# A hybrid decoder layer: the feed-forward parts, the values and the output projection with tokens held in the matmul engine

## The chip, the cores and the metric

The kernel runs on one core of a Trainium2 chip. The metric is the device time of one execution in microseconds (us). The engines are TensorE (PE; its weight loads stand as PEld), VectorE (DVE), ScalarE (ACT), GpSimd (POOL) and SyncE (SP), which issues the DMAs here. The inputs, all in f32, lie in the chip's memory.

## The reference

One layer for 256 tokens of width 1024. A vector `c` gives, by a 1024 x 9216 matrix (`ada`), nine rows of 1024: shift, scale and gate for each of three blocks. The blocks are a SwiGLU feed-forward part of width 2816 (FFN1, with half a step), a mixer and a second feed-forward part (FFN2).

```
def rmsnorm(x, g):  return x * rsqrt(mean(x * x, -1) + EPS) * g
def modulate(h, shift, scale):  return h * (1 + scale) + shift
def swiglu(h, w_gate, w_up, w_down):  return (silu(h @ w_gate) * (h @ w_up)) @ w_down
...
proj = h @ w_in                       # q, k, v of 512 columns each, x_m and z of 512 each
o_a = rmsnorm(attention of 8 heads of 64)
o_m = (norm of an mLSTM of 4 heads of 128 + skip * conv) * silu(z)
return concatenate([o_a, o_m]) @ w_out
```

Each block is x + gate * block(modulate(rmsnorm(x))), the gates of the feed-forward parts halved; a last norm with `final_norm` follows.

## The kernel before, in words

**Weights.** All weights come once, as 1 MB chunks of 128x2048 in four buffers named `raw`. `load_to` issues their DMAs on SyncE's queue, three chunks ahead of use (`weights(ahead=3)`). Each chunk is cut in pieces of 1024 columns, and each piece is split in two parts: ScalarE writes the rounded `whi`, VectorE the rest, `wlo = raw - whi` (`split_piece`), one chunk ahead of use. Five buffers hold each part.

**Products.** Activations are kept with features on the partitions, as `hh` and `hl` (rounded and rest). `mm3` makes a product of three matmuls: `whi` with `hh`, `wlo` with `hh`, `whi` with `hl`. A 128x128 block of the weights rests in TensorE, and 256 columns, the tokens, pass through. The result has features on the partitions and tokens along the columns.

**Norms.** `residual` adds a block's result to x by features (one piece of 128 features x 256 tokens at a time), squares it, and makes the next `hh` and `hl` at once with `pre_h`, without the norm's factor. The factor, one number per token, is made meanwhile from sums of squares over the partitions by a plain f32 matmul with ones (`rstd_of`), and is multiplied in behind the next product (`finish_pre`, `shifted`, `conv`). The shift passes through the product as two more columns (W = 258 columns, `pre_shift`).

**FFN.** Gate and up columns are produced tile by tile (22 tiles of 128), the gated product `gm` is split in `gh` and `gl`, and the down projection makes 8 tiles of 128 features, each a sum over 22 blocks.

**Adaptive rows.** The 72 columns of `c @ ada` are made on VectorE: a 128x1024 tile `ada` is loaded (three buffers) and multiplied with the broadcast `c_bc` with a running sum (`junk<-ada,c_bc`). The first 16 come before FFN1, the others are put in one by one with `side`: `QF` and `QD` say how many by chunk in FFN1's gate/up and down parts.

**Order.** DMAs on SyncE and the loads of ScalarE's tables stand as written. The order of the other engines is set by the tile framework's scheduler, which moves instructions by its own timeline; each engine then runs its list in order, and waits are by semaphore.

## Time and profile before

| | us |
|---|---|
| median of three runs | 546.89 |
| lowest and highest | 544.8, 547.9 |
| the profiled execution | 544.78 |
| its span | 543.0 |
| FFN1 gate/up, full stretch | 41.8 to 147.4 |
| FFN1 down | 147.4 to 209.8 |
| mixer | 209.8 to 313.7 |
| output projection | 313.7 to 338.6 |
| FFN2 gate/up | 338.6 to 469.7 |
| FFN2 down | 469.7 to 531.9 |
| tail | 531.9 to 543.0 |

A stretch's busy time of an engine is to be held against the stretch's length: where TensorE's equals it, TensorE sets the pace, and other engines' waits cost nothing. A matmul's recorded duration is its latency, and matmuls overlap; the pace is the distance from one start to the next, or the chain's length over its count. In a group of several records, the time runs from the first start to the last end.

### The profile page before, as it was taken

The page shows a single profiled execution, that of the slowest core. Times are in us where ns is not written, and L with a number is a line of the kernel's source. Part 1 is how long each engine was busy: PE and PEld are TensorE (multiplying, and loading weights), DVE is VectorE, ACT ScalarE, POOL GpSimd, SP SyncE. Part 2 cuts the span into 40 slices and gives each one's busy share as a digit, 9 for nine tenths or more (in the row PEclk, how much of TensorE's full clock was granted, in tenths as well). Part 3 has the DMA queues.
Part 4 walks back from the last instruction along what each step waited for, and adds up shares of the span by engine and source line. Part 5 has one row for each costly group of instructions (what it writes and reads, how often), then busy time and mean ns, then how long its engine had stood idle before and what let it go on. Part 6 is the DMA issues. An engine that isn't in the chain of part 4 may idle for free.

```text
span 543.0 us, 10281 instructions
## 1 busy us (share of the span) xinstructions
PE 520.8 (96%) x4172; PEld 502.2 (92%) x4172; DVE 419.6 (77%) x712; ACT 281.6 (52%) x486; POOL 48.8 (9%) x64
## 2 busy tenths in 40 slices
PE   7799999899999999999999979999999999999992
PEld 7799999899999999988977779999999999999992
DVE  7989879999889887998965286989987777644423
ACT  4455346456655345366767554875554554544410
POOL 4000000000001010210000030400000000023221
PEclk9999999999999999999999989999999999999998
DMA  8998987879779889579621114387856455455002
GB/s 312 341 415 324 367 307 299 319 305 332 295 278 320 326 278 348 216 269 349 228 79 59 31 73 150 124 354 278 316 182 218 160 172 217 156 189 200 1 0 77
DMA packets 23953, 125.76 MB, mean 232 GB/s; under 512 B 2657, under 2 KB 2913, under 8 KB 14434
## 3 DMA queue, kind: packets, MB, share of 16 engines
q1 hardware_dynamic: 23906, 125.11, 62.5%
q8 instruction: 32, 0.52, 0.4%
q14 instruction: 15, 0.12, 0.1%
HBM read 124.05 MB, written 1.05 MB: 230 GB/s over the span
## 4 chain that ended last, share of the span: by engine, by line
PE 90%; DVE 5%; DMA 2%; ACT 1%; issue 1%; SPq 0%; DVEq 0%; ACTq 0%
PE psa L54 42%; PE psb L54 26%; PE psm L54 22%; DVE junk L54 2%; DMA raw<-in_gu 1%; DMA x<-in_x 1%; DVE wlo L54 1%; DVE u_out L54 0%; ACT whi L54 0%; DVE nw L54 0%; DVE oa L54 0%; ACT sq L54 0%; SPq L97 0%; DVEq L1080 0%; DVE rr L54 0%
## 5 line engine op out<-in xcount | busy, mean ns | idle before, releaser
L54 ACT ACTIVATE whi<-raw 128x1024 fp32r<-128x1024 f32 (+1 forms) x162 | 169.2, 1048 | 137.5 <-PE psa L54 65.1
L54 DVE TENSOR_TENSOR wlo<-raw,whi 128x1024 fp32r<-128x1024 f32 (+1 forms) x162 | 196.2, 1215 | 53.3 <-ACT whi L54 52.2
L54 PE MATMUL psa<-hh,whi 128*128 128x258 f32 (+1 forms) x396 | 110.4, 283 | 0.6 <-DVE gm L54 0.6
L54 PE MATMUL psa<-hh,wlo 128*128 128x258 f32 (+1 forms) x396 | 110.5, 283 | 0.0
L54 PE MATMUL psa<-hl,whi 128*128 128x258 f32 (+1 forms) x396 | 109.4, 283 | 0.0
L54 PE MATMUL psb<-hh,whi 128*128 128x258 f32 (+1 forms) x320 | 92.1, 289 | 4.3 <-ACT whi L54 2.4
L54 DVE SCALAR_TENSOR_TENSOR junk<-ada,c_bc 128x1024 bf16<-128x1024 f32 x72 | 87.7, 1218 | 8.9 <-DMA ada<-in_ada 8.7
L54 PE MATMUL psb<-hh,wlo 128*128 128x258 f32 (+1 forms) x320 | 90.5, 284 | 1.2 <-DVE wlo L54 1.2
L54 PE MATMUL psb<-hl,whi 128*128 128x258 f32 (+1 forms) x320 | 90.0, 284 | 0.0
L54 PEld LDWEIGHTS psa<-hh,whi 128*128 128x128 f32 x396 | 74.4, 189 | 0.8 <-DVE gm L54 0.8
L54 PEld LDWEIGHTS psa<-hh,wlo 128*128 128x128 f32 x396 | 74.4, 189 | 0.0
L54 PEld LDWEIGHTS psa<-hl,whi 128*128 128x128 f32 x396 | 74.0, 190 | 0.0
L54 PEld LDWEIGHTS psb<-hh,whi 128*128 128x128 f32 x320 | 60.4, 189 | 6.8 <-ACT whi L54 3.0
L54 PEld LDWEIGHTS psb<-hh,wlo 128*128 128x128 f32 x320 | 60.3, 189 | 2.0 <-DVE wlo L54 1.4
L54 PEld LDWEIGHTS psb<-hl,whi 128*128 128x128 f32 x320 | 60.3, 190 | 0.0
L54 PE MATMUL psm<-hh,wlo 128*128 128x256 f32 (+1 forms) x204 | 57.4, 283 | 0.0
L54 PE MATMUL psm<-hh,whi 128*128 128x256 f32 (+1 forms) x204 | 57.3, 283 | 0.0
L54 PE MATMUL psm<-hl,whi 128*128 128x256 f32 (+1 forms) x204 | 57.0, 283 | 0.0
L54 PE MATMUL psa<-gh,whi 128*128 128x256 f32 x176 | 49.5, 281 | 0.0
L54 PE MATMUL psa<-gh,wlo 128*128 128x256 f32 x176 | 49.5, 281 | 0.0
L54 PE MATMUL psa<-gl,whi 128*128 128x256 f32 x176 | 49.4, 281 | 0.0
L54 PEld LDWEIGHTS psm<-hh,whi 128*128 128x128 f32 x204 | 38.5, 189 | 0.1
(235 smaller groups left out, 903.8 us busy)
## 6 DMA issues: line engine op xcount, KB each, us to landing
ada<-in_ada SPq DMA_DIRECT2D x72, 512.0 KB, 5.8
raw<-in_dn SPq DMA_DIRECT2D x22, 1024.0 KB, 4.8
raw<-in_guB SPq DMA_DIRECT2D x19, 1024.0 KB, 4.7
raw<-in_gu SPq DMA_DIRECT2D x18, 1024.0 KB, 6.4
raw<-in_gu SPq DMA_DIRECT2D x8, 512.0 KB, 7.3
raw<-in_wqk SPq DMA_DIRECT2D x4, 1024.0 KB, 5.6
raw<-in_wout SPq DMA_DIRECT2D x4, 1024.0 KB, 7.9
raw<-in_guA SPq DMA_DIRECT2D x4, 768.0 KB, 4.4
```

Source lines behind the costliest of these rows:

```text
L54: r = f(*a, **k)
```

## The change

In the feed-forward parts, the values and the output projection the roles are turned: `mx3` rests a block of 128 features x 128 tokens (`tok`) in TensorE, and 512 columns of weights pass through. The result has tokens on the partitions. The products of q, k, x_m and z stay as `mm3`, with 256 columns instead of 258.

- x is kept by tokens (`xt`, two tiles of 128 x 1024; `turn_x` makes them with transposes). `residual` multiplies a 128x512 result by the gate as a row and adds; ScalarE sums the squares along the row. `row_norm` makes the factor per token with a power on GpSimd. `normed` makes y = x * factor * scale row + shift row, and `to_h` turns y by transposes and splits it in `hh` and `hl`. The norm's factor is thus applied ahead of the products of the mixer and FFN2.
- The gated product comes by tokens too (`gated`), and `turn` transposes it into `gh` and `gl`.
- The gate, scale and shift rows and the final norm are written to a scratch in memory (`row_of`, 128x8x1) and read back broadcast over the partitions (`load_row`, 128x1024).
- The columns of the down weights are regrouped: a chunk holds 4 or 2 row blocks x 512 columns (`down`, SIZES) and is loaded in four or five DMAs of 256 KB or less. Some pairs of gate/up chunks and the values' chunks are loaded in two DMAs each.
- In FFN1's down part 24 of the `ada` jobs run (16 before): QF, QD = (1, 0, 1), (2, 0, 0).

The core of the diff:

```diff
+    def by_row(g, d):
+        def pieces(raw):
+            v = raw.rearrange("p (g d c) -> p d g c", g=g, d=d)
+            n = d * 1024 // raw.shape[-1]
+            return [v[:, k:k + n] for k in range(0, d, n)]
+        return pieces
...
+    def down(src, dg, a, n):
+        def moves(raw):
+            r = []
+            for k in range(4):
+                b, o = (4 * dg + k) * NF + a, k * n * P
+                while o < (k + 1) * n * P:
+                    m = min((k + 1) * n - o // P, 16 - b % 16)
+                    r.append((raw[:, o:o + m * P], src[b // 16][:, b % 16 * P:(b % 16 + m) * P]))
+                    b, o = b + m, o + m * P
+            return r
+        return 4 * n * P, moves, by_row(4, n)
+    SIZES = [4, 4, 4, 2, 4, 4]
+    def downs(src):
+        return [down(src, dg, sum(SIZES[:k]), n) for dg in range(2) for k, n in enumerate(SIZES)]
...
+    def mx3(ps, xh, xl, hi, lo, start, stop):
+        pe.matmul(ps, xh, hi, start=start, stop=False, skip_group_check=True)
+        pe.matmul(ps, xh, lo, start=False, stop=False, skip_group_check=True)
+        pe.matmul(ps, xl, hi, start=False, stop=stop, skip_group_check=True)
...
+    def row_of(src, name):
+        scr = scratch[name] = drm.tile([ND, P], F32, name=nm("scr"), tag=nm("scr"))
+        later.append((jobs_run[0] + 1, lambda: dma(scr.rearrange("j p -> p j"), src)))
+    def run_later(all=False):
+        while later and (all or later[0][0] <= jobs_run[0]):
+            later.pop(0)[1]()
+    def load_row(name, tag):
+        rows[name[:2]] = const([P, D], F32, "row", tag=tag)
+        dma(rows[name[:2]], scratch[name].rearrange("j p -> (j p)").partition_broadcast(P))
...
-    def pre_h(k, d):
-        act.activation(hh[:, d, 0:T], x_sb[:, d], AF.Copy, scale=gs[k][:, d:d + 1])
-        dve.scalar_tensor_tensor(hl[:, d, 0:T], x_sb[:, d], gs[k][:, d:d + 1], as32(hh[:, d, 0:T]),
-                                 ALU.mult, ALU.subtract)
-    def pre_shift(k):
-        for c in range(2):
-            act.activation(hh[:, :, T + c], sh[k], AF.Copy)
-            dve.tensor_tensor(hl[:, :, T + c], sh[k], as32(hh[:, :, T + c]), ALU.subtract)
...
-    def residual(d, ps, g, k):
-        dve.scalar_tensor_tensor(x_sb[:, d], ps, g[:, d:d + 1], x_sb[:, d], ALU.mult, ALU.add)
-        if k is None:
-            s = add_sq(d, pool)
-            pool.tensor_scalar(fin_u[0][:, d], x_sb[:, d], sm[:, C_NF + d:C_NF + d + 1], None, ALU.mult)
-            return s
-        if d == ND - 1:
-            s = add_sq(d, pool)
-            pre_h(k, d)
-        else:
-            pre_h(k, d)
-            s = add_sq(d, pool)
-        return s
-    fin_u = [None]
...
+    def residual(k, tt, dg, ps):
+        c = slice(dg * 512, dg * 512 + 512)
+        t = t512("rt")
+        x = xt[tt][:, c]
+        dve.tensor_tensor(t, ps, rows["gt"][:, c], ALU.mult)
+        dve.tensor_tensor(x, x, t, ALU.add)
+        n = 4 * k + 2 * tt + dg
+        t2 = tmp.tile([P, 512], BF16, tag="sq5", name=nm("sq5"), bufs=1)
+        act.activation(t2, x, AF.Square, accum_out=ss[:, n:n + 1])
+    def row_norm(k, tt):
+        n, m = 4 * k + 2 * tt, 2 * k + tt
+        dve.tensor_scalar(rt[:, m:m + 1], ss[:, n:n + 1], ss[:, n + 1:n + 2], D * EPS, ALU.add, ALU.add)
+        pool.tensor_tensor(rt[:, m:m + 1], rt[:, m:m + 1], mhalf, op=ALU.pow)
+        return rt[:, m:m + 1]
+    def normed(k, tt):
+        r = row_norm(k - 1, tt)
+        ys = []
+        for dg in range(2):
+            c = slice(dg * 512, dg * 512 + 512)
+            y = t512("y", bufs=4)
+            dve.scalar_tensor_tensor(y, xt[tt][:, c], r, rows["gs"][:, c], ALU.mult, ALU.mult)
+            dve.tensor_tensor(y, y, rows["sh"][:, c], ALU.add)
+            ys.append(y)
+        return ys
+    def to_h(tt, ys, tag="b"):
+        for dg, y in enumerate(ys):
+            pt = bank(tag)
+            for d in range(4):
+                pe.transpose(pt[:, d * P:(d + 1) * P], y[:, d * P:(d + 1) * P], ident)
+            v = pt.rearrange("p (d t) -> p d t", d=4)
+            o = (slice(None), slice(dg * 4, dg * 4 + 4), slice(tt * P, tt * P + P))
+            act.activation(hh[o], v, AF.Copy)
+            dve.tensor_tensor(hl[o], v, as32(hh[o]), ALU.subtract)
+    def tok(x, d, tt):
+        return x[:, d, tt * P:(tt + 1) * P]
...
+    def gated(g, u, n):
+        s = t256("sl")[:, 0:n * P].rearrange("p (f c) -> p f c", f=n)
         act.activation(s, g, AF.Silu)
-        m = t256("gm")
-        dve.tensor_tensor(m, s, u, ALU.mult)
-        hilo(gh[:, ft], gl[:, ft], m)
-    def finish_pre(gh, gl, ft, g, u, r):
-        c = tmp.tile([P, 1], F32, tag="col", name=nm("col"), bufs=3)
-        act.activation(c, g[:, T:T + 1], AF.Copy)
-        t = t256("ht", bufs=3)
-        dve.tensor_tensor(t, r, g[:, 0:T], ALU.mult)
-        s = t256("sl")
-        act.activation(s, t, AF.Silu, bias=c)
-        t2 = t256("ht", bufs=3)
-        dve.tensor_tensor(t2, r, u[:, 0:T], ALU.mult)
-        m = t256("gm")
-        dve.scalar_tensor_tensor(m, t2, u[:, T:T + 1], s, ALU.add, ALU.mult)
-        hilo(gh[:, ft], gl[:, ft], m)
-    ring = ["b", "m", "a", "a", "b", "m", "a", "a"]
-    def ffn(k, nxt):
-        nfa = 3
+        m = t256("gm", bufs=6)[:, 0:n * P]
+        dve.tensor_tensor(m.rearrange("p (f c) -> p f c", f=n), s, u, ALU.mult)
+        return m
...
+                def turn():
+                    pt = bank()
+                    for q in range(n):
+                        for tt in range(2):
+                            pe.transpose(pt[:, q * T + tt * P:q * T + (tt + 1) * P], ms[tt][:, q * P:(q + 1) * P],
+                                         ident)
+                    v = pt[:, 0:n * T].rearrange("p (f t) -> p f t", f=n)
+                    act.activation(gh[:, f:f + n], v, AF.Copy)
+                    dve.tensor_tensor(gl[:, f:f + n], v, as32(gh[:, f:f + n]), ALU.subtract)
...
+            def half_rows(w, ps, d0, first=False):
+                for tt in range(2):
+                    for d in range(4):
+                        mx3(ps[tt], tok(hh, d0 + d, tt), tok(hl, d0 + d, tt), *part(w, d * 512, 512),
+                            start=(d == 0 and (d0 == 0 or first)), stop=(d == 3))
...
+            def rows_of(w, n, a, dg, tts):
+                for f in range(n):
+                    for tt in tts:
+                        mx3(pd[tt], tok(gh, a + f, tt), tok(gl, a + f, tt), *part(w, f * 512, 512),
+                            start=(a + f == 0), stop=(a + f == NF - 1))
+            for dg in range(2):
+                pd = [bank() for _ in range(2)]
+                a = 0
+                for q, n in enumerate(SIZES):
+                    if dg == 1 and q == 4:
+                        ws = []
+                        for _ in range(2):
+                            ws.append(weights())
+                            side(QD[k])
+                        for tt in range(2):
+                            for q2, w in enumerate(ws):
+                                rows_of(w, 4, a + 4 * q2, dg, (tt,))
+                        break
+                    w = weights()
+                    side(QD[k])
+                    rows_of(w, n, a, dg, (0, 1))
+                    row_loads(k, dg, q)
+                    while turns:
+                        turns.pop(0)()
+                    a += n
+                if dg == 0:
+                    for tt in range(2):
+                        residual(k, tt, 0, pd[tt])
+            for tt in range(2):
+                residual(k, tt, 1, pd[tt])
...
+    ROWS = {(0, 0, 2): ("gt0", "H2"), (0, 1, 1): ("gs1", "x0"), (0, 1, 2): ("sh1", "x1"),
+            (2, 0, 4): ("gt2", "H2"), (2, 1, 1): ("nf", "H3")}
+    def row_loads(k, dg, q):
+        if (k, dg, q) in ROWS:
+            run_later(True)
+            load_row(*ROWS[k, dg, q])
+    QF, QD, jobs = (1, 0, 1), (2, 0, 0), []
...
+    jobs += gate_jobs(0) + scale_jobs(1) + shift_jobs(1) + gate_jobs(1) + scale_jobs(2) + shift_jobs(2)
+    ffn(0)
+    ys = [normed(1, tt) for tt in range(2)]
...
-    def shifted(dst):
+    def copied(dst):
         def done(pb):
-            col = tmp.tile([P, 1], F32, tag="col", name=nm("col"), bufs=3)
-            act.activation(col, pb[:, T:T + 1], AF.Copy)
-            t = t256("ht", bufs=3)
-            dve.tensor_tensor(t, r, pb[:, 0:T], ALU.mult)
-            act.activation(dst, t, AF.Identity, bias=col)
+            act.activation(dst, pb[:, 0:T], AF.Copy)
         return done
...
+    def values():
+        pv = [bank("a") for _ in range(2)]
+        for h in range(2):
+            w = weights()
+            for tt in range(2):
+                for d in range(4):
+                    mx3(pv[tt], tok(hh, 4 * h + d, tt), tok(hl, 4 * h + d, tt), *part(w, d * 512, 512),
+                        start=(d == 0 and h == 0), stop=(d == 3 and h == 1))
+            if h == 1:
+                for tt in range(2):
+                    act.activation(va[:, tt], pv[tt], AF.Copy)
+            yield
...
+    def out_rows(k, w, tt):
+        xh, xl = (v[:, tt * P:(tt + 1) * P] for v in mix(k))
+        for dg in range(2):
+            b0 = k % 2 * 1024 + dg * 512
+            mx3(po[tt][dg], xh, xl, *part(w, b0, 512), start=(k == 0), stop=(k == 7))
```

How the rows move. VectorE at the border from FFN1 to the mixer, before (`x` is the last residual, `hl` the last operand made from it):

```order
L54 SCALAR_TENSOR_TENSOR x<-psa_2553,gt_157,x 128x256
L54 MEMSET xm_2789 128x4x3
L54 TENSOR_SCALAR rows_2794<-maskt 36x256
L54 TENSOR_TENSOR wlo_2720<-raw_2572,whi_2719 128x1024
L54 SCALAR_TENSOR_TENSOR hl<-x,gs_152,hh 128x256
L54 TENSOR_TENSOR wlo_2724<-raw_2572,whi_2723 128x1024
L54 SCALAR_TENSOR_TENSOR junk_2656,mod<-ada_2654,c_bc 128x1024
L54 SCALAR_TENSOR_TENSOR nw_2677<-rr_2673 128x256
```

and after (`psp_1687` is the last sum of FFN1's second 128 tokens, `xt` the residual, `y` the normed rows):

```order
L54 TENSOR_TENSOR rt_1946<-psp_1687,row_1547 128x512
L54 MEMSET xm_1982 128x4x3
L54 TENSOR_SCALAR rows_1987<-maskt 36x256
L54 TENSOR_TENSOR gt_161<-mod,b_152 128x8
L54 TENSOR_TENSOR wlo_2064<-raw_1856,whi_2063 128x1024
L54 SCALAR_TENSOR_TENSOR junk_1868,mod<-ada_1866,c_bc 128x1024
L54 TENSOR_TENSOR xt_1273<-xt_1273,rt_1946 128x512
L54 TENSOR_TENSOR wlo_2068<-raw_1856,whi_2067 128x1024
L54 TENSOR_SCALAR rt_167<-ss 128x1
L54 SCALAR_TENSOR_TENSOR junk_1873,mod<-ada_1871,c_bc 128x1024
L54 TENSOR_SCALAR rt_167<-ss 128x1
L54 SCALAR_TENSOR_TENSOR y_1954<-xt_1266,rt_167,row_1779 128x512
```

Where one residual and one hl stood between two splits, there is now a chain of residual, norm and four y, with splits and accumulations of adaLN between its steps.

TensorE at the same place, before:

```order
L54 MATMUL psa_2553<-gl_167,whi_2500 128x256
L54 MATMUL psa_2553<-gh_166,whi_2500 128x256
L54 MATMUL psa_2553<-gh_166,wlo_2501 128x256
L54 MATMUL psa_2553<-gl_167,whi_2500 128x256
L54 MATMUL psa_2640<-hh,whi_2574 128x258
L54 MATMUL psa_2640<-hh,wlo_2575 128x258
L54 MATMUL psa_2640<-hl,whi_2574 128x258
L54 MATMUL psa_2641<-hh,whi_2574 128x258
```

and after (`psb` are the transposed y, `wif` and `raw` the fold of the gates' weights, `psa_2057` the first product of the mixer):

```order
L54 MATMUL psp_1687<-whi_1862,gl_174 128x512
L54 MATMUL psb_2002<-ident,y_1954 128x128 x4
L54 MATMUL psb_2009<-ident,y_1957 128x128 x4
L54 MATMUL psa_2030<-wif_1979,raw_1977 128x40 x11
L54 MATMUL psb_2016<-ident,y_1962 128x128 x4
L54 MATMUL psb_2023<-ident,y_1965 128x128 x4
L54 MATMUL psa_2030<-wif_1979,raw_1977 128x40
L54 MATMUL psa_2044<-raw_1977 128x128 x4
L54 MATMUL psa_2057<-hh,whi_1877 128x256
L54 MATMUL psa_2057<-hh,wlo_1878 128x256
L54 MATMUL psa_2058<-hh,whi_1877 128x256
L54 MATMUL psa_2058<-hh,wlo_1878 128x256
```

The first product with `hh` came right behind the last with `gl`; now 16 transposes and the fold stand between them, and the first product with `hl` needs the third group of transposes, split on VectorE.

SyncE in FFN1's down part, before:

```order
L97 DMA raw_1939<-in_dn 128x2048
L97 DMA ada_1949<-in_ada 128x1024
L97 DMA ada_1953<-in_ada 128x1024
L97 DMA raw_2012<-in_dn 128x2048
L97 DMA ada_2022<-in_ada 128x1024
L97 DMA raw_2081<-in_dn 128x2048
L97 DMA ada_2091<-in_ada 128x1024
L97 DMA ada_2095<-in_ada 128x1024
```

and after (`scr` is the scratch, `row` a broadcast row):

```order
L104 DMA ada_1701<-in_ada 128x1024
L104 DMA scr_1651<-sh_158 128x8x1
L104 DMA ada_1706<-in_ada 128x1024
L104 DMA raw_1734<-in_dn 128x512 x4
L104 DMA ada_1747<-in_ada 128x1024
L104 DMA ada_1751<-in_ada 128x1024
L104 DMA row_1779<-scr_1479 128x1024
L104 DMA raw_1781<-in_dn 128x512 x4
L104 DMA ada_1790<-in_ada 128x1024
L104 DMA ada_1794<-in_ada 128x1024
```

A chunk of down weights was one DMA and is now four, there are two loads of `ada` to each chunk, and a scatter and the broadcast rows stand in the same queue.

## Rows read from the trace of the kernel before

**Rows 1.** The page: busy time by engine; the chain's shares.
```profile
PE 520.8 (96%) x4172; PEld 502.2 (92%) x4172; DVE 419.6 (77%) x712; ACT 281.6 (52%) x486; POOL 48.8 (9%) x64
...
PE 90%; DVE 5%; DMA 2%; ACT 1%; issue 1%; SPq 0%; DVEq 0%; ACTq 0%
```

**Rows 2.** Stretches; columns: window, length, busy PE, PEld, DVE, ACT, POOL, PEclk, DMA share, GB/s.
```profile
41.80:147.40 105.60, 103.87 (x866) 103.47 (x865) 95.83 (x161) 54.19 (x83) 0.00 (x0) 1.00 0.84 320
...
147.40:209.80 62.40, 62.40 (x530) 62.40 (x529) 54.19 (x78) 31.26 (x43) 5.40 (x7) 1.00 0.83 298
...
240.00:313.70 73.70, 71.66 (x492) 57.88 (x491) 50.89 (x123) 46.38 (x123) 3.21 (x4) 1.00 0.43 154
...
313.70:320.00 6.30, 4.64 (x24) 4.44 (x25) 5.71 (x13) 3.97 (x8) 3.33 (x3) 0.73 0.01 3
...
531.90:543.00 11.10, 1.11 (x4) 0.31 (x3) 4.95 (x10) 1.30 (x3) 2.51 (x3) 0.77 0.26 94
```

**Rows 3.** The chain of waits: start, length, work.
```profile
163.09 15.62 PE psa L54 x132
...
359.46 5.79 PE psm L54 x48
```

**Rows 4.** Timeline of TensorE at 5.6 us: start, length, operation.
```profile
5.41 0.40 PE L54 MATMUL psm<-c_hl,ones_r 128*128 128x512 f32 x1
5.65 0.61 PE L54 MATMUL psa<-ones_m 128*128 128x128 f32 x4
```

**Rows 5.** Timeline of TensorE at 213.7 us, a plain f32 product among others.
```profile
213.69 0.59 PE L54 MATMUL psm<-sq,ones_m 128*128 128x256 f32 x2
213.93 0.47 PE L54 MATMUL psa<-hl,whi 128*128 128x258 f32 x1
214.24 0.29 PE L54 MATMUL psa<-hh,whi 128*128 128x258 f32 x1
```

**Rows 6.** Timeline of TensorE in the mixer, transposes.
```profile
266.62 0.27 PE L54 MATMUL psa<-ident,pr 128*128 128x128 f32 x1
...
266.85 0.49 PE L54 MATMUL psa<-ident,pr 128*128 128x128 f32 x3
```

**Rows 7.** The stretch of the highest DMA rate, columns as in rows 2.
```profile
20.00:40.00 20.00, 16.50 (x131) 15.87 (x132) 18.40 (x30) 10.69 (x14) 0.00 (x0) 1.00 1.01 391
```

**Rows 8.** Groups by line and form: count, busy, mean ns, idle before.
```profile
L54 DVE TENSOR_TENSOR wlo<-raw,whi 128x1024 fp32r<-128x1024 f32 x158 | 193.7, 1229 | 52.8 <-ACT whi L54 51.7
...
L54 DVE SCALAR_TENSOR_TENSOR junk<-ada,c_bc 128x1024 bf16<-128x1024 f32 x72 | 87.7, 1218 | 8.9 <-DMA ada<-in_ada 8.7
...
L54 POOL TENSOR_TENSOR acc<-acc,sq 128x256 f32<-128x256 f32 x20 | 20.4, 1020 | 64.1 <-ACT sq L54 63.8
...
L54 DVE SCALAR_TENSOR_TENSOR x<-psa,gt,x 128x256 f32<-128x256 f32 x12 | 5.6, 477 | 13.1 <-PE psa L54 13.0
...
L54 DVE TENSOR_TENSOR half<-half,psa 128x512 f32<-128x512 f32 x4 | 2.7, 679 | 0.0
```

**Rows 9.** Timeline of TensorE at the border from FFN1 to the mixer.
```profile
209.66 0.28 PE L54 MATMUL psa<-gl,whi 128*128 128x256 f32 x1
209.78 0.28 PE L54 MATMUL psa<-hh,whi 128*128 128x258 f32 x1
```

**Rows 10.** Timeline of TensorE, the fold of the gates.
```profile
227.98 2.77 PE L54 MATMUL psa<-wif,raw 128*128 128x40 f32 x24
```

**Rows 11.** Timeline of TensorE at the output projection's start; idle before in brackets.
```profile
315.86 0.53 PE L54 MATMUL psm<-mix0l,whi 128*128 128x256 f32 x1 [1.42 <-DVE mix0l L54]
316.18 0.42 PE L54 MATMUL psm<-mix0h,whi 128*128 128x256 f32 x1
316.40 0.41 PE L54 MATMUL psm<-mix0h,wlo 128*128 128x256 f32 x1
```

**Rows 12.** The page's DMA issues: count, KB each, us to landing.
```profile
raw<-in_dn SPq DMA_DIRECT2D x22, 1024.0 KB, 4.8
...
ada<-in_ada SPq DMA_DIRECT2D x72, 512.0 KB, 5.8
```

More of the change, by code (lines that the diff above doesn't have):

```diff
@@ L22 @@
 NF = 22
-W = T + 2
 NH = 4
@@ L182, in layer, with chunk, cut, pair @@
-    raws, parts, used = [], [], [0]
+    def chunk(src, pieces=None):
+        n = src.shape[-1]
+        return n, lambda raw: [(raw, src)], pieces or (lambda raw: cut(raw))
+    def cut(v, n=1024):
+        return [v[..., k:k + n] for k in range(0, v.shape[-1], n)]
+    def pair(src, f, h):
+        def moves(raw):
+            v = raw.rearrange("p (f c) -> p f c", f=2)
+            return [(v[:, k], src[f + k][:, h * 1024:(h + 1) * 1024]) for k in range(2)]
+        return 2048, moves, by_row(2, 4)
@@ L269, in shift_fin @@
         dve.tensor_tensor(sh[k][:, a:b], mod[:, s0 + a:s0 + b], sm[:, s0 + a:s0 + b], ALU.add)
+        if k:
+            row_of(sh[k], f"sh{k}")
     def ada_jobs(col, fin):
-        r = [lambda on, c=c: ada(col + c, on) for c in range(8)]
+        r = [lambda c=c: ada(col + c) for c in range(8)]
         last = r[7]
-        r[7] = lambda on: (last(on), fin())
+        r[7] = lambda: (last(), fin())
         return r
@@ L559, in layer, with ready @@
[L559 to L571 removed]
+                def ready(g):
+                    finish(8 + 2 * g, 2, [view(p) for p in ps[g]])
@@ new lines, in ffn @@
+            if k:
+                w = weights()
+                pb = [bank() for _ in range(2)]
+                for tt in range(2):
+                    for d in range(8):
+                        mx3(pb[tt][:, 0:T], tok(hh, d, tt), tok(hl, d, tt), *part(w, d * T, T),
+                            start=(d == 0), stop=(d == 7))
+                while turns:
+                    turns.pop(0)()
+                finish(NF - 1, 1, [view(p, 1) for p in pb])
+            def rows_of(w, n, a, dg, tts):
[3 more added lines that the diff above has]
+                            start=(a + f == 0), stop=(a + f == NF - 1))
@@ new lines, in layer @@
+    with tc.tile_pool(name="ps2", bufs=1, space=bass.MemoryType.PSUM) as p2:
+        banks[0] = (p2, True)
+        with tc.tile_pool(name="mix", bufs=1) as mp:
+            mixer(tc, nc, i, mp, locals())
+    with tc.tile_pool(name="ps3", bufs=1, space=bass.MemoryType.PSUM) as p3:
+        banks[0] = (p3, False)
+        jobs += gate_jobs(2)
+        ys = [normed(2, tt) for tt in range(2)]
+        to_h(0, ys[0])
+        nf = const([P, ND], F32, "nf")
+        dve.tensor_scalar(nf, sm[:, C_NF:C_NF + 8], ROOT, None, ALU.mult)
+        row_of(nf, "nf")
+        ffn(2, lambda: to_h(1, ys[1]))
+        for tt in range(2):
+            r = row_norm(2, tt)
+            for dg in range(2):
+                c = slice(dg * 512, dg * 512 + 512)
+                y = t512("y", bufs=4)
+                dve.scalar_tensor_tensor(y, xt[tt][:, c], r, rows["nf"][:, c], ALU.mult, ALU.mult)
+                pt = bank()
+                for d in range(4):
+                    pe.transpose(pt[:, d * P:(d + 1) * P], y[:, d * P:(d + 1) * P], ident)
+                o = t512("rt")
+                act.activation(o, pt, AF.Copy)
+                sp.dma_start(out[:, dg * 4:dg * 4 + 4, tt * P:(tt + 1) * P], o.rearrange("p (d t) -> p d t", d=4))
@@ L902, in a_out @@
                 hilo(*mix(0), o)
-    side(1, 0)
+    for tt in range(2):
+        to_h(tt, ys[tt])
+    fold()
+    px = [bank("a") for _ in range(4)]
+    for c in range(2):
+        w = weights()
+        side(1)
+        for d4 in range(4):
+            d = c * 4 + d4
+            for h in range(NH):
+                mm3(px[h][:, 0:T], w, d4 * 512 + h * P, hh[:, d], hl[:, d], start=(d == 0), stop=(d == 7))
+    side(1)
     g = queries(0)
@@ L943, in mixer @@
     m_scores(2)
-    g0 = values(1)
-    side(0, 1)
-    next(g0)
+    side(1)
     weigh(1)
```

483 lines of the change are left out of this document (239 added, 244 removed).

## The prediction

> **What bounds the kernel now.** I read the page's shares first, then the stretches by engine, then the chain of waits. TensorE is busy 96% of the span and carries 90% of the chain [rows 1]. By stretch: FFN1's gate/up part (41.8 to 147.4 us) is full but for some 2 us, with VectorE at 95.8 of 105.6 us and the DMA share at 0.84; FFN1's down part (to 209.8) has no idle time, at DMA share 0.83 and 298 GB/s; the mixer (240 to 313.7) leaves TensorE 2 us of recorded idle, and its weight loads are busy 57.9 of 73.7 us where in the full stretches they are busy all the time, so more idle time is hidden in matmuls that wait; the tail after the last matmul is 11.1 us [rows 2]. So every us of TensorE counts, and slack is nowhere large. All sums are made against the profiled execution: 544.8 us, span 543.0, which is 2.1 below the median of 546.9.
>
> **The change part by part.**
>
> *The stream.* Before, 2304 wide matmuls have 256 columns and 1536 have 258 (1152 of them in FFN2's gate/up and the values, which the change turns; 384 in q, k, xm, z, which stay but lose two columns). One costs 15.62/132 = 118.3 ns at 256 and 5.79/48 = 120.6 ns at 258 [rows 3]. The turned part is 2304 x 0.1183 + 1152 x 0.1206 = 411.5 us. After, the same products are 1680 matmuls of 512 columns and 96 of 256. Their pace decides the case, and 512 columns of this type appear twice in the trace, in the broadcast of c: the second starts at 5.41 and what follows it at 5.65, 0.235 to 0.24 us later, and the 128-column records behind run 0.11 apart, which is the full-clock pace [rows 4]. That is twice 118.3 within a percent. The other bound is the plain f32 matmul: of 213.69, two records, then the queued 258-column one, and the next starts at 214.24, so (0.55 - 0.12)/2 = 0.215 a record [rows 5], and a record there passes its 256 columns twice. I take 0.235, since that row has the same type and width as the new stream: 1680 x 0.235 + 96 x 0.1183 = 406.2, that is -5.3; the 384 that lose two columns give 384 x 0.0023 = -0.9. Together **-6.2 us**, and -39 at 0.216.
>
> The Trainium skill ("TensorE: Matmul & The Clock Gate", section "Back-to-back issue gap") gives N/2.4 + 2.5 ns for N streamed columns. At 256 this would be 109 ns, where the trace has 118.3, so the rule doesn't hold here for this type; at 512 it would be 215.8 and the stream would shrink by some 38 us.
>
> *Transposes.* 88 turn the gated product into the down projection's operand, 48 turn the normalised rows y, 16 turn x, and 8 of the values go: +144. Three in a row take 0.49 us and one alone 0.27, so one step is 0.11 us [rows 6]. TensorE is the bound, so all of it counts: **+15.8 us**. The matmuls of the column sums for the norms go (3 norms, 2 products of 2 records at 0.215): **-2.6**.
>
> *FFN1's down part.* Its order of issue on SyncE now has 24 jobs of adaLN (16 before), the weights in pieces of 128x512, a scatter and two broadcast rows. 11 MB of weights, 12 MB of ada, 1.5 of rows are 24.5 MB in TensorE's 62.4 us; before it was 298 x 62.4 = 18.6 MB at a share of 0.83 [rows 2]. At the best rate the trace shows (391 GB/s, 20 to 40 us, share 1.0 [rows 7]) it takes 62.7 us; at that stretch's own share per byte, 0.83 x 62.4 x 24.5/18.6 = 68. The queue is in order and the fourth raw buffer hides one chunk. I take **+2** (0.5 to 6). VectorE there does 22 splits and 24 accumulations, at 1.23 and 1.22 us [rows 8], and about 6 us of residual: 62 by durations, a little less since neighbours overlap; it fits, just.
>
> *The border from FFN1 to the mixer.* Before there is no stall: the first product with hh starts 0.12 us behind the last with gl [rows 9], because the norm's factor is applied behind the matmul. Now the rows must be normed first, then turned. VectorE runs in order, and its order behind the last psp (the piece of the order shown) has, until the hl of the third group that TensorE needs: 3 splits of weights, 5 accumulations of adaLN, the residual's product and sum, 4 products and 4 sums of y, 3 hl, the fold of the values' weights. By rows: 3 x 1.23 + 5 x 1.22 + (2 + 4 + 3) x 0.68 = 15.9; the four products of y have no row at 512 columns, between 0.48 (256 columns, same operation) and 1.22 (1024), I take 0.7, +2.8; the small ones (memset, mask, factors, fold of the values) I put at 2; less an overlap of neighbours of some 0.7: **20 us**. POOL's power on 128x1 has no row either: between nothing and the 1.02 us of a 128x256 sum there [rows 8]; I take 0.5, beside VectorE's queue. What TensorE has meanwhile: 16 transposes 1.8, the fold of the gates with 32 records at 2.77/24 = 0.115, that is 3.7 [rows 10], 4 matmuls 0.5, together 6.0. Idle **+14**: the splits and accumulations are work that VectorE owes anyway, but its order puts them ahead of what TensorE waits for. Range 6 (if the splits and accumulations ran in the time when VectorE waits for the last sum) to 20.
>
> *The border from the mixer to FFN2.* The same with less in between: 3 splits of 128x768 (0.93 each by 1.23 x 3/4), 4 passes of the residual, 4 products of y, 3 sums, 1 hl ahead of the first product with hl; by those durations 10 us, less some 1 of overlap, TensorE having 12 transposes and 4 matmuls (2 us) meanwhile: **+7** (4 to 11).
>
> *The clock.* Before the out projection, where TensorE had idled 1.42 us, its matmuls run 0.22 apart instead of 0.12 [rows 11]; the stretch's granted clock is 0.73 of 2.4 GHz over 6.3 us [rows 2], which is 3.4 us at the lower of its two levels, 1.2 GHz, and costs 1.7. Each of the two new waits is longer than that one: **+3** (0 to 3).
>
> *What else goes.* In the mixer the multiplication by the norm's factor and the copies of the shift columns (38 and 37 operations on VectorE and ScalarE) go, and with them waits of TensorE there: 2 us are recorded, and the 15.8 us in which the weight loads aren't busy hold an unknown part more; I take **-5** (0 to -8). The tail: before 11.1 us; now two passes of the residual 1.4, square and factor 1.2, product 0.7, turn and copy 1.1, seams 0.4, and some 5 for the last DMA and the end as before: about 9.8, **-1.3** (0 to -3). The start keeps its norm by features: 0. The scatters of 128x8x1 lie off the path; they cost nothing if SyncE isn't held by them, which is a rival.
>
> Sum: -6.2 + 15.8 - 2.6 + 2 + 14 + 7 + 3 - 5 - 1.3 = +26.7; 544.8 + 26.7 = **571 us**.
>
> **The rivals.**
> *A, the wide stream is really faster.* If 512 columns take 0.216 us, the overhead per matmul being what the narrow form pays, the stream gives 32 us more: 571 - 32 = 539, faster by 1%. For it: the f32 records [rows 5]. Against: the one row of the same type [rows 4]. With cheap borders too it would be near 525.
> *B, half of that.* 256 columns at 2.4 GHz are 106.7 ns; if the 11.6 ns above it are fixed, 512 take 213.3 + 11.6 = 225: -17, 554. The row of 0.235 is against it, by more than its rounding.
> *C, the borders are cheap.* If VectorE and ScalarE come to the border with no backlog, and TensorE gets its first operand after 12 us instead of 20 at the one and after 5 less at the other, and the clock stays up: 571 - 8 - 5 - 3 = 555. For it: VectorE has idle time in FFN1's down part before. Against: its order as written.
> *D, DMA decides in FFN1's down part.* The queue gets 256 KB pieces with lines of 2 KB, scatters of 4 bytes and broadcast rows, all in order. Before, 1 MB of weights lands in 4.8 us and 512 KB of ada in 5.8 [rows 12], and the stretch has 17% of its DMA time to spare. If the new form costs a fifth of the best rate, 391 x 0.8 = 313 GB/s, the 24.5 MB take 78 us, 16 more than TensorE's 62.4 where the sum has 2: 585. It decides from 391 GB/s downwards, since 62.7 us is already TensorE's own time. For it: VectorE too is nearly full there. Against: the weights are 11 of the 24.5 MB, the rest comes as before.
>
> The Trainium skill ("DMA: Bandwidth & Descriptors", its section of rates measured from HBM to SBUF) has 341 GB/s for transfers of 1 MB and 138 for 64 KB, and asks for at least 1 MB a transfer; no run here shows the new sizes, and it speaks for D.
>
> **How the numbers follow.** The forecast as it stands has 0.50, its own range 560 to 582. A has 0.13, B 0.09, C 0.14, D 0.14. A measurement of this kernel can tell about 0.5% (2.7 us) from no change. Faster by more: A, and 0.02 of C where the stream is also faster: 0.15. No change: 0.04 of B and 0.03 of C, where the two meet or the mixer gives back its 8: 0.07. Slower: 0.50 + 0.14 + 0.05 of B + 0.09 of C = 0.78. The range reaches from A's 539 to a little beyond D's 585: 538 to 588.
>
> **What would show it.** Right: wide matmuls 0.23 to 0.24 us apart in FFN2's chain of waits; TensorE idle 10 us or more before the first mixer product, released by VectorE's hl; 5 us or more at FFN2's start, and the clock low behind both; 0.11 a transpose; a down part of FFN1 near 66 us with its transposes. Wrong: a pace of 0.216 (A), borders under 6 us together (C), raw or row pieces as what TensorE's splits wait for over 10 us in the down part (D), or a mixer that gives back over 10 us.

## The result, and the profile after

The changed kernel takes 623.0 us in the median (622.6 to 623.7, four runs) against 547.0 before: a ratio of 1.139 [1.136, 1.143]. The forecast was 571, with a range of 538 to 588. The sign was right, the size far off: +76 us instead of +24.

The page of the changed kernel, shares by engine and the chain's, to be held against [rows 1]:

```profile
PE 539.3 (87%) x2624; PEld 438.7 (71%) x2624; DVE 400.9 (65%) x629; ACT 267.0 (43%) x409; POOL 24.0 (4%) x40
...
PE 51%; DMA 26%; DVE 12%; issue 4%; SPq 3%; ACT 3%; POOL 0%; POOLq 0%; DVEq 0%; ACTq 0%
```

DMA had 2% of the chain and now has 26%. TensorE is no longer the bound. The stretches, with the columns of [rows 2], cut at FFN1's first and last product with `gh`, the first transpose of y, the last product of the output projection, the first transpose of FFN2's y and the last product of all:

```profile
0.00:155.00 155.00, 144.59 (x649) 116.65 (x649) 120.95 (x200) 75.76 (x103) 6.01 (x21) 0.98 0.78 280
155.00:242.80 87.80, 67.06 (x270) 52.34 (x268) 51.35 (x69) 23.15 (x27) 0.00 (x0) 0.90 0.73 239
242.80:266.20 23.40, 0.39 (x2) 0.00 (x0) 14.43 (x27) 4.40 (x7) 1.78 (x4) 0.60 0.60 156
266.20:405.00 138.80, 130.33 (x792) 108.39 (x792) 94.36 (x185) 74.33 (x152) 11.15 (x11) 0.93 0.59 179
405.00:411.70 6.70, 0.00 (x0) 0.03 (x1) 6.25 (x12) 2.53 (x7) 3.07 (x2) 0.71 0.48 155
411.70:611.00 199.30, 194.43 (x901) 159.61 (x902) 110.54 (x135) 83.80 (x109) 1.43 (x2) 0.98 0.60 175
611.00:620.90 9.90, 2.50 (x17) 1.68 (x15) 3.01 (x5) 3.00 (x6) 0.55 (x1) 0.75 0.35 106
```

Against before: FFN1 up to the down part +8, the down part +25 (87.8 for 62.4), the border +23, mixer and output projection +10, the second border +7, FFN2 +6, the tail -1. That is the 77.9 us between the two spans. In the down part TensorE is idle for 21 us although the DMA share is only 0.73 and the rate 239 GB/s, less than before: the loads are late without the DMA engines being full. Who waits for loads, from the view of waits (total us, times, longest):

```profile
DVE junk L54 <- DMA ada<-in_ada: 85.0, 23, 10.5
...
ACT whi L54 <- DMA raw<-in_dn: 39.1, 5, 15.6
```

The place to look at is SyncE's queue at one scatter (start, us, operation), and the DMA rate behind it in steps of 2 us:

```profile
173.25 0.38 SPq L104 DMA_DIRECT2D scr<-gs  x1
173.67 0.58 SPq L104 DMA_DIRECT2D ada<-in_ada  x1
174.29 1.41 SPq L104 DMA_DIRECT2D row<-scr  x1
175.81 3.19 SPq L104 DMA_DIRECT2D raw<-in_dn  x5
185.14 1.62 SPq L104 DMA_DIRECT2D ada<-in_ada  x2
```

```profile
174.00:176.00 2.00, 2.00 (x10) 1.63 (x9) 2.00 (x3) 0.54 (x2) 0.00 (x0) 1.00 0.42 43
176.00:178.00 2.00, 2.00 (x11) 1.65 (x10) 1.34 (x3) 0.91 (x1) 0.00 (x0) 1.00 0.11 14
178.00:180.00 2.00, 2.00 (x11) 1.65 (x10) 0.00 (x0) 0.00 (x0) 0.00 (x0) 1.00 0.19 35
180.00:182.00 2.00, 1.47 (x7) 0.89 (x5) 0.00 (x0) 0.00 (x0) 0.00 (x0) 1.00 0.24 31
182.00:184.00 2.00, 0.00 (x0) 0.00 (x0) 0.00 (x0) 0.00 (x0) 0.00 (x0) 1.00 0.50 35
```

A scatter is the write of one row of 4 KB to the scratch (128x8x1). Behind this one the whole core loads at 14 to 43 GB/s for 10 us, and at the end all engines stand still. There are eight scatters, and the rate falls behind each of them.

The stream itself is near the forecast. 512-column matmuls in FFN2's gate/up part:

```profile
500.01 0.39 PE L54 MATMUL psp<-whi,hh 128*128 128x512 f32 x1
500.24 0.40 PE L54 MATMUL psp<-wlo,hh 128*128 128x512 f32 x1
500.48 0.40 PE L54 MATMUL psp<-whi,hl 128*128 128x512 f32 x1
```

They start 0.235 apart, as the one row of before had it [rows 4]; over all 1618 pairs of neighbours the median is 0.233. That median mixes two paces, since the down projections run faster (nine steps lie between these two rows):

```profile
579.62 0.39 PE L54 MATMUL psp<-whi,gh 128*128 128x512 f32 x1
...
581.66 0.39 PE L54 MATMUL psp<-whi,gh 128*128 128x512 f32 x1
```

That is 0.227 a matmul, the median of the down projections' pairs, against 0.234 in the rest. Rival A (0.216) is out. Rival B's 0.225 is out for the gate/up part, but the 528 matmuls of the two down projections, of 1680, come within 1% of it. The Trainium skill ("TensorE: Matmul & The Clock Gate", section "Back-to-back issue gap") has N/2.4 + 2.5 ns for the gap of an isolated matmul, 0.216 here; for this type both measured paces lie above it.

### The profile page after: what moved, and what is told of

Same layout as the page of the kernel before. It is cut to its first block, busy times and chain, and to the rows that moved or that the text cites. A ratio compares the mean times of both kernels' runs of the same rounds, so it can differ in the third digit from the quotient of the medians.

```text
span 620.9 us, 7242 instructions
## 1 busy us (share of the span) xinstructions
PE 539.3 (87%) x2624; PEld 438.7 (71%) x2624; DVE 400.9 (65%) x629; ACT 267.0 (43%) x409; POOL 24.0 (4%) x40
## 4 chain that ended last, share of the span: by engine, by line
PE 51%; DMA 26%; DVE 12%; issue 4%; SPq 3%; ACT 3%; POOL 0%; POOLq 0%; DVEq 0%; ACTq 0%
PE psp L54 37%; DMA ada<-in_ada 13%; PE psa L54 8%; PE psb L54 5%; DVE wlo L54 5%; DMA raw<-in_dn 4%; SPq L104 3%; DVE junk L54 3%; DMA wif<-in_wif 3%; DMA scr<-gs 2%; PE psm L54 1%; DMA raw<-in_wxm 1%; DMA raw<-in_gu 1%; ACT whi L54 1%; DVE rt L54 1%
## 5 line engine op out<-in xcount | busy, mean ns | idle before, releaser
L54 PE MATMUL psp<-whi,hh 128*128 128x512 f32 (+1 forms) x368 | 143.4, 398 | 4.3 <-ACT hh L54 3.1
L54 PE MATMUL psp<-wlo,hh 128*128 128x512 f32 (+1 forms) x368 | 143.5, 393 | 2.7 <-DVE wlo L54 2.7
L54 PE MATMUL psp<-whi,hl 128*128 128x512 f32 (+1 forms) x368 | 139.4, 389 | 0.0
L54 PE MATMUL psp<-wlo,gh 128*128 128x512 f32 x176 | 70.9, 404 | 17.8 <-DVE wlo L54 17.8
L54 PEld LDWEIGHTS psp<-whi,hh 128*128 128x128 f32 x368 | 70.2, 192 | 20.8 <-ACT hh L54 3.8
L54 PEld LDWEIGHTS psp<-wlo,hh 128*128 128x128 f32 x368 | 70.5, 192 | 18.5 <-DVE wlo L54 3.6
L54 PEld LDWEIGHTS psp<-whi,hl 128*128 128x128 f32 x368 | 69.6, 190 | 14.9
L54 PE MATMUL psp<-whi,gh 128*128 128x512 f32 x176 | 70.4, 401 | 1.3 <-ACT whi L54 1.3
L54 PE MATMUL psp<-whi,gl 128*128 128x512 f32 x176 | 70.1, 399 | 0.0
L54 PEld LDWEIGHTS psp<-wlo,gh 128*128 128x128 f32 x176 | 34.2, 194 | 27.5 <-DVE wlo L54 20.6
```

What stands on the lines that cost most here:

```text
L54: r = f(*a, **k)
```

## The experiments

Thirteen kernels, on two questions: what the DMAs cost (1 to 5, 7, 8, 12), and what the borders cost (6, 9 to 11, 13). The runs of before beside them have medians of 546.7 to 547.4. The expectations go by theories: S, the scatters slow the loads; P, the pieces of the down weights do; O, VectorE's order makes the waits at the borders, against W, what stands in that order is owed anyway and comes back behind the border.

**1. The scatters' lines.** The changed kernel with rows written as 32-byte lines:

```diff
-        scr = scratch[name] = drm.tile([ND, P], F32, name=nm("scr"), tag=nm("scr"))
-        later.append((jobs_run[0] + 1, lambda: dma(scr.rearrange("j p -> p j"), src)))
+        scr = scratch[name] = drm.tile([P, ND], F32, name=nm("scr"), tag=nm("scr"))
+        later.append((jobs_run[0] + 1, lambda: dma(scr, src)))
...
+        rows[name[:2]] = row.rearrange("p (t d) -> p d t", d=ND)
```

> Changed kernel with each of the eight rows written to the scratch as 128 lines of 32 bytes instead of 1024 lines of 4 bytes (the broadcast row is then read by VectorE with a stride). Theory S (scatters): in the trace of the changed kernel the DMA rate falls to 14 to 43 GB/s for 8 to 11 us behind each scatter, so eight of them hold some 70 us of the queue, most of it in stretches where TensorE waits for loads; the time falls from 623 to 555 to 580 us. Theory P (pieces: the down weights in 256 KB pieces with 2 KB lines are what slows the loads): 610 to 625. Theory O (order of VectorE at the borders, which waits nowhere on DMA): 605 to 625.

Measured: 588.7 us, 34 under the changed kernel; ratio to before 1.076 [1.074, 1.078]. That is theory S by the mechanism, 9 us outside its range, and neither P nor O. The page's count of DMA packets and its DMA issues (KB each, median us to landing), of the changed kernel and then of this one:

```profile
DMA packets 55909, 129.80 MB, mean 209 GB/s; under 512 B 12865, under 2 KB 19777, under 8 KB 52546
...
scr<-gt SPq DMA_DIRECT2D x3, 4.0 KB, 11.4
```

```profile
DMA packets 48741, 129.80 MB, mean 221 GB/s; under 512 B 5697, under 2 KB 12609, under 8 KB 45378
...
scr<-gt SPq DMA_DIRECT2D x3, 4.0 KB, 1.4
```

The packets under 512 bytes fall by 8 x (1024 - 128) = 7168, for the same megabytes.

**2. The pieces.** One DMA for each chunk of down weights:

```diff
         def moves(raw):
+            return [(raw, src[5 * dg + a // 4][:, 0:4 * n * P])]
```

> Changed kernel with each chunk of down weights loaded by one DMA of 128x2048 (or 128x1024), the same bytes; the columns are then not regrouped, so the down projection multiplies with other weights. Theory P: 585 to 600. Theories S and O: 615 to 623.

Measured: 611.3 us, 12 under the changed kernel; between the theories, closer to S. The columns are not regrouped here, so this kernel and that of run 4 show the time and not the layer's result.

**3. The scatters alone, in the kernel before.**

```diff
+    def row_of(src, name):
+        scr = drm.tile([ND, P], F32, name=nm("scr"), tag=nm("scr"))
+        later.append((jobs_run[0] + 1, lambda: dma(scr.rearrange("j p -> p j"), src)))
...
+        row_of(gt[k], f"gt{k}")
```

> Kernel before with the same eight scatters of 128x8x1 added at the same places of its job list; nothing reads them. Theory S: each costs up to 10 us less what the loads are ahead (one to three chunks of 3 to 6 us); 547 becomes 575 to 610. Theory P and O: 545 to 550.

Measured: 599.2 us, ratio 1.098 [1.092, 1.104]. Eight writes of 4 KB that nobody reads cost 52 us. Their landing, as in the changed kernel:

```profile
scr<-gt SPq DMA_DIRECT2D x3, 4.0 KB, 11.8
```

**4. Both edits.**

> The two edits of the first two kernels together (the down weights again not regrouped). Theory S: within 5 us of the first. Theory P: within 5 us of the second. If both cost something: 20 us or more under the better of the two. Theory O: above 600.

Measured: 577.8 us, 11 under the first and 34 under the second. The two add up: scatters 34, pieces 11 to 12. The 20 us that the expectation asked for if both cost something were more than the pieces cost.

**5. The pieces, with the right weights.** The regrouped order is laid out in memory, so that a chunk is one DMA.

```diff
         def moves(raw):
...
+            return [(raw, src[6 * dg + q][:, 0:4 * n * P])]
...
+                v = dn[4 * dg:4 * dg + 4, at:at + m]
+                blocks[6 * dg + q, :, 0:4 * m * P] = v.transpose(2, 0, 1, 3).reshape(P, 4 * m * P)
```

> The kernel with 32-byte lines (588.7 us) with the down weights laid out regrouped in memory, so that each chunk is one DMA and the result stays. Theory S with pieces as a second cost: 574 to 582, like the run that left the columns where they were (577.8). If that run gained by anything but the pieces: 585 to 590.

Measured: 578.8 us (574.5 to 583.0), ratio 1.059 [1.051, 1.067], as forecast there. Its four runs spread over 8.5 us, so differences of a few us from this kernel are not clear of noise. Its stretches, cut at the same places:

```profile
150.00:210.20 60.20, 60.20 (x270) 49.80 (x268) 49.74 (x65) 23.91 (x28) 0.00 (x0) 1.00 0.89 346
210.20:224.30 14.10, 0.31 (x2) 0.00 (x0) 13.78 (x23) 4.14 (x7) 2.15 (x4) 0.65 0.67 267
224.30:357.80 133.50, 128.90 (x792) 107.10 (x792) 95.39 (x185) 73.00 (x150) 11.29 (x11) 0.95 0.49 179
357.80:367.60 9.80, 0.18 (x1) 0.02 (x1) 9.35 (x14) 3.70 (x10) 3.45 (x2) 0.67 0.35 110
367.60:561.20 193.60, 192.43 (x901) 158.38 (x902) 114.34 (x135) 83.41 (x109) 1.83 (x2) 0.99 0.53 179
```

FFN1's down part ends at 210.2 where it ended at 209.8 before, with the changed kernel's 24 jobs of adaLN in it, now at 346 GB/s. The border is 14.1 us, the second one 9.8, FFN2 lasts 193.6 against 193.3. What is left of the loss is in the main the borders and the mixer. The pieces cost in FFN1: in run 1's trace its down part takes 67.2 us, here 60.2, while FFN2's down part takes 60.0 in both.

**6. The order at both borders.** VectorE and ScalarE pinned to program order:

```diff
+            dve.on = act.on = True
             for tt in range(2):
                 residual(k, tt, 1, pd[tt])
+                if k == 0:
+                    ys.append(normed(1, tt))
```

> As e5_pack, with VectorE and ScalarE held to program order at both borders, so that no split or accumulation of later chunks stands between the residual, the norm, y and hl; y of the first 128 tokens is made before the residual of the second. Theory O (the order of VectorE makes the two border waits): TensorE's wait behind FFN1 falls from some 14 us to 3 to 7, the one ahead of FFN2 from 10 by 1 to 4, and the time is 10 to 18 us under e5_pack. Rival W (what stands there is owed anyway, and comes back as waits for splits right behind): within 4 us of e5_pack.

Measured: 594.0 us, 15 slower. Neither theory. VectorE's timeline (start, us, operation, idle before and its cause) shows why:

```profile
215.45 1.23 DVE L54 SCALAR_TENSOR_TENSOR junk<-ada,c_bc 128x1024 bf16<-128x1024 f32 x1 [2.50 <-DMA ada<-in_ada]
...
219.44 1.22 DVE L54 SCALAR_TENSOR_TENSOR junk<-ada,c_bc 128x1024 bf16<-128x1024 f32 x1 [2.75 <-DMA ada<-in_ada]
...
223.81 1.23 DVE L54 SCALAR_TENSOR_TENSOR junk<-ada,c_bc 128x1024 bf16<-128x1024 f32 x1 [3.14 <-DMA ada<-in_ada]
...
224.96 1.06 DVE L54 TENSOR_TENSOR rt<-psp,row 128x512 f32<-128x512 f32 x1
```

The pinned residual stood behind accumulations whose loads were not there yet; TensorE waited 23 us. The last row shows a second thing: with a row read at a stride the product takes 1.06 us. The mean of eight is 686 ns in the changed kernel, where the row lies in a line, and 1114 in e5_pack:

```profile
L54 DVE TENSOR_TENSOR rt<-psp,row 128x512 f32<-128x512 f32 x8 | 5.3, 686 | 6.8 <-PE psp L54 6.8
```

```profile
L54 DVE TENSOR_TENSOR rt<-psp,row 128x512 f32<-128x512 f32 x8 | 8.8, 1114 | 5.8 <-PE psp L54 5.8
```

**7. The 32-byte lines in the kernel before.** The edit of 1 on the kernel of 3.

```diff
-        scr = drm.tile([ND, P], F32, name=nm("scr"), tag=nm("scr"))
-        later.append((jobs_run[0] + 1, lambda: dma(scr.rearrange("j p -> p j"), src)))
+        scr = drm.tile([P, ND], F32, name=nm("scr"), tag=nm("scr"))
+        later.append((jobs_run[0] + 1, lambda: dma(scr, src)))
```

> Kernel before with the eight writes to the scratch in 128 lines of 32 bytes, where 1024 lines of 4 bytes gave 599 us. If the number of lines is what costs: 547 to 555. If it is that a small write with a wait stands in SyncE's queue at all: 580 to 600.

Measured: 544.8 us, ratio 0.996 [0.995, 0.998]. The same eight writes of 4 KB cost nothing; the form in 1024 lines of 4 bytes is what costs. The number of lines and their length change together here, and no run parts them. The Trainium skill ("DMA: Bandwidth & Descriptors", section "Specifications") puts the least transfer for full rate at 512 bytes; the lines of both forms lie under that bound, so it doesn't tell them apart.

**8. Another queue.**

```diff
-        later.append((jobs_run[0] + 1, lambda: dma(scr.rearrange("j p -> p j"), src)))
+        later.append((jobs_run[0] + 1, lambda: act.dma_start(scr.rearrange("j p -> p j"), src)))
```

> Changed kernel with the eight scatters of 4-byte lines issued by ScalarE instead of SyncE, else the same. If the scatter costs because the loads stand behind it in one queue: 585 to 600, near the kernel with 32-byte lines. If its lines occupy the DMA engines themselves, whatever the queue: 615 to 630.

Measured: 601.8 us, 21 under the changed kernel, between the two ranges. The scatter still lands after 12.9 us, and while it runs, the loads in SyncE's queue are slow too:

```profile
136.00:138.00 2.00, 2.00 (x11) 1.59 (x10) 0.00 (x0) 1.02 (x1) 0.00 (x0) 1.00 1.14 19
138.00:140.00 2.00, 2.00 (x12) 1.62 (x11) 1.66 (x3) 1.59 (x3) 0.00 (x0) 1.00 0.58 8
```

So the queue's order is a part of the cost and what both queues share another. The Trainium skill ("DMA: Bandwidth & Descriptors", section "Queues, rings and completion order") says that each DMA engine takes turns between the queues by packets; these rows, with 19 and 8 GB/s, don't speak against that and don't show it either.

**9. Rows turned on TensorE**, written as 8 lines of 512 bytes and read without a stride:

```diff
+            pe.transpose(pt[0:ND, 0:P], src, ident)
...
+            act.activation(st, pt[0:ND, 0:P], AF.Copy)
+            dma(scr, st)
```

> As e5_pack (578.8 us), but each row is turned on TensorE to 8x128 and written as 8 lines of 512 bytes, so that VectorE reads the broadcast row without a stride. In the trace of e6_order the products and sums with a strided row take 1.06 to 1.19 us where the rows of before give 0.68 for 512 columns in a line; 4 gates, 4 y and 4 sums stand on each border. If that counts: 2 to 8 us under e5_pack. If VectorE's order alone sets the border: within 2 us.

Measured: 582.5 us (577.0 to 584.7), 4 above e5_pack: the time is inconclusive on the stride, since a new wait came in (see 10). The border to FFN2 does show it. TensorE's wait there, in e5_pack and then here:

```profile
367.61 2.03 PE L54 MATMUL psp<-ident,y 128*128 128x128 f32 x8 [9.62 <-DVE y L54]
```

```profile
378.46 1.94 PE L54 MATMUL psp<-ident,y 128*128 128x128 f32 x8 [6.93 <-DVE rt L54]
```

The wait is 2.7 us shorter without the stride. Runs 1 and 4, with it, wait 9.6 us too, and the changed kernel and runs 10 and 11, without it, 6.8 to 6.9.

**10. The order again**, on 9, with the accumulations of FFN1's last three chunks moved into the mixer, where five calls of `side` take two instead of one. The pinning is that of 6, for the first border alone.

```diff
-                            side(QD[k])
+                            side(0 if k == 0 else QD[k])
...
-                    side(QD[k])
+                    side(0 if dg == 1 and q == 3 else QD[k])
```

> As e9_turned_lines, with VectorE and ScalarE held to program order at the border from FFN1 to the mixer, y of the first tokens ahead of the residual of the second, and the accumulations of adaLN of FFN1's last three chunks moved into the mixer (e6_order pinned the residual behind four of them, which waited for their loads until 224.96 us). Theory O: TensorE's wait there falls from 14 us to 3 to 7, the time is 6 to 14 us under e9. Rival W (the moved work comes back as waits in the mixer): within 3 us of e9.

Measured: 579.4 us (576.8 to 581.2), 3 under e9 with ranges that overlap. TensorE's timeline has the border (idle before in brackets) at 5.55 us in run 9, where nothing was moved or pinned yet:

```profile
233.74 1.94 PE L54 MATMUL psb<-ident,y 128*128 128x128 f32 x8 [5.55 <-DVE y L54]
```

and in this run at 4.87, behind another wait:

```profile
191.62 0.37 PE L54 MATMUL psp<-ident,sh 128*8 128x128 f32 x1 [9.26 <-DVE sh L54]
...
228.34 1.97 PE L54 MATMUL psb<-ident,y 128*128 128x128 f32 x8 [4.87 <-DVE rt L54]
```

The transpose of the shift row stands in TensorE's order and waits for the last accumulation of that row, 11.0 us in run 9 and 9.3 here, inside FFN1's down part. So the border's fall from 14 us came with this wait, in run 9, and can't be put down to the move or the order. What the move is worth shows over both: from FFN1's first down product to the mixer's first product with `hh` it is 94.0 us in run 9, with 4.4 of a wait for the load of `wif` in them, and 87.1 here.

**11. Moved, not pinned:** 10 without `dve.on = act.on = True`, with y behind both residuals again.

> As e10_order without the pinned order: the accumulations are moved, the scheduler orders the rest. Theory O: between e9 and e10, the wait 8 to 12 us, since three or four splits still stand between the steps. If the accumulations alone made the wait: equal to e10.

Measured: 576.9 us (575.8 to 578.4); the wait at the border is 3.9 us, no longer than in e10, and from FFN1's first down product to the mixer's first with `hh` it is 87.0 us, as there. So against theory O the pinned order adds nothing to the move, though splits still stand between the steps. The time is under e9's by 6 us, and the ratios to before, 1.055 [1.051, 1.058] and 1.064 [1.059, 1.069], don't overlap.

**12. The pieces in the kernel before.**

```diff
-            cuts = 1 if len(raws) > 3 else 2
+            cuts = 4 if len(raws) in DOWN else 1 if len(raws) > 3 else 2
```

> Kernel before with each chunk of down weights loaded in four DMAs of 128x512 (256 KB, lines of 2 KB), the same bytes in the same order. If the pieces cost the 11 us by their rate, hidden in before by 17% of spare DMA time and one to three chunks of lead: 546 to 551. If four issues in SyncE's queue hold up what stands behind them: 552 to 560.

Measured: 547.9 us, ratio 1.004 [1.002, 1.006]. Hidden there; in the changed kernel, whose queue is short of time in FFN1, they cost 10 to 12.

**13. The order of 10 on 5**, with nothing on TensorE for the rows.

> As e5_pack (32-byte lines, rows read with a stride, nothing on TensorE for the rows), with the order and the moved accumulations of e10_order. Theory O: TensorE's wait behind FFN1 falls from 14.1 us to 5 to 8 and the time by 6 to 12 us, to 567 to 573. Rival W (the moved accumulations come back as waits in the mixer or ahead of the output projection): 575 to 581.

Measured: 573.6 us (571.7 to 576.8), 5 under e5_pack by the medians, with ranges that overlap, and between theory O and rival W. The two waits of TensorE:

```profile
219.89 1.97 PE L54 MATMUL psb<-ident,y 128*128 128x128 f32 x8 [6.60 <-DVE rt L54]
...
330.40 0.79 PE L54 MATMUL psa<-whi,mix0h 128*128 128x512 f32 x1 [8.09 <-ACT mix0h L54]
```

TensorE's wait at the border fell from 14.0 to 6.6 us, with a down part as long as in e5_pack, and some of it came back ahead of the output projection, where e5_pack hardly waits; that kernel has two waits of 2.8 and 1.2 later on, which are gone here. It has the lowest median of these versions and is still 5.0% slower than before; none beats before.

## Why the prediction was wrong

*The step that failed* is "The scatters of 128x8x1 lie off the path; they cost nothing if SyncE isn't held by them", together with the +2 for FFN1's down part. No DMA that the kernel before issues writes lines of 4 bytes, so no row gave a price, and it was put at nothing instead of being bounded. The condition was met and it cost all the same: SyncE issued the scatter at 173.25 us in 0.38 us and went on to the next load at 173.67. What was held were the loads behind it. Each scatter slows them for some 10 us; alone in the kernel before, the eight cost 52 us (run 3), and in the changed kernel their lines cost 34 (run 1), a net figure, since the remedy makes VectorE's operations on rows longer. Rival D named them, and the sign that it gave came true (of the 39.1 us in which `whi` waits for `raw`, 37.5 lie in the down part), but it took them as a fifth off the best rate in FFN1's down part alone, 585 us. They took nine tenths off it for 10 us at a time, in five stretches of the program. The broadcast rows, which D named too, stand in run 5 as well, where TensorE has no idle time in the down part. D had 0.14, and the upper end of the range rested on its 585.

*The pieces* were part of the same term, +2 with a range of 0.5 to 6, and cost 10 (run 5 against 1). In before they are hidden (run 12), and in FFN2's down part too: they cost only in FFN1, where the queue is late.

*The stream* (-6.2) was right in its choice of a row, which decided the sign: 0.234 a matmul for 0.235. For the down projections it was too slow; with their 0.227 the turned part is 528 x 0.227 + 1152 x 0.234 + 96 x 0.1183 = 400.8 us for the 406.2 of the sum, 5 us more to gain. (At 0.216 the term would have been -38 and not -39.)

*The transposes and the whole of TensorE's work* were right in sum. FFN2, with 44 of the product's transposes, lasts 193.6 us in run 5 against 193.3. FFN1 ends at 210.2 against 209.8 before; its 60 transposes (+6.6), its stream (-1.3) and the +2 of its down part were to make some 7.

*The border to the mixer* (+14) is 14.1 in run 5, without the scatters, and 23.4 in the changed kernel, where a scatter stands in it and VectorE waits 9.0 us for a load of `ada`. The number came out in part by luck, since the chain ended elsewhere. TensorE waits for y, and not for hl, and behind the transposes it works without a pause until the mixer's first product:

```profile
224.49 2.03 PE L54 MATMUL psb<-ident,y 128*128 128x128 f32 x8 [13.98 <-DVE y L54]
...
234.60 0.51 PE L54 MATMUL psa<-hh,whi 128*128 128x256 f32 x1
```

Those 10 us of work were put at 6.0 and run at the lower clock. That the accumulations in VectorE's order are a part of the wait is borne out: with them moved the time from FFN1's first down product to the mixer's first product with `hh` falls by 7 us, without pinning (87.0 for 94.0, run 11 against 9) as with it (77.5 for 84.7, run 13 against 5).

*The border to FFN2* (+7) is 6.7 in the changed kernel, and 9.8 in run 5 where the rows are read at a stride. The durations listed for it add up to 11.0 and not to 10, so the same working gives +8.

*The clock* (+3) was mis-sized. In run 5 the window behind the border, in the columns of [rows 2]:

```profile
224.40:240.00 15.60, 15.51 (x92) 15.31 (x93) 13.94 (x25) 4.49 (x7) 0.00 (x0) 0.66 0.84 299
```

TensorE works all the time, and the granted clock is 0.66 on the average of 15.6 us: 15.6 x 0.34 = 5.3 us lost, against 1.7 in [rows 2, 11]. Those 1.7 stood behind two waits and not the one of 1.42 us that the prediction names; 1.9 us ahead of it the trace of before has

```profile
313.94 0.39 PE L54 MATMUL psm<-mix0h,whi 128*128 128x256 f32 x1 [2.28 <-ACT mix0h L54]
```

*The mixer* (-5) was wrong. From the border to the end of the output projection run 5 takes 133.5 us, and 128.8 before. The 4.7 us more are about those 5.3 of the clock and 0.9 for eight more transposes, which leaves -1.5 for the work that went. Waits are no shorter: 2.8 and 1.2 us ahead of the output projection's end, where before had 2.28 and 1.42.

*The tail* (-1.3) came out at -1.2: 9.9 against 11.1 us; in run 5, with the stride, it is 12.0.

Without the two DMA costs the sum comes near: 571 forecast, 577.8 and 578.8 measured in runs 4 and 5. That is luck in part, since errors of both signs cancel in it: in run 5 FFN1 is some 7 us better than its terms, the mixer with its clock and both the second border and the tail are worse.

## What to carry to other kernels

An operation that the trace of before doesn't show must not be priced at nothing because it is off the path: look at the number and length of its lines, not only at its bytes, and ask what stands behind it in the queue and in the DMA engines. Turning a matmul round saves little here, since the pace per column is nearly the same (0.46 to 0.47 ns before, 0.44 to 0.46 after), and it costs transposes and a norm that stands ahead of the product; the waits at such a border are found in the order of the engine that makes the operand, and work that waits for loads is the first to move out of there. Here that took 7 us off the border, of which a part came back later.
